# A sixth seven-product pair in five gate and up units, and where the unit before is turned back

## The chip, the cores and the metric

One core of a Trainium2 chip runs the whole program. TensorE (PE, with its weight loads PEld) multiplies, VectorE (DVE) and ScalarE (ACT) work on what it reads and leaves, GpSimd (POOL) and SyncE (SP) issue DMAs. The metric is the device time of one execution in microseconds (us). Lower is better.

## What is computed

The reference is a decoder layer on 16 + 256 tokens of width 2048: a gated feed-forward block (FFN1), attention beside a short convolution, a gated merge, a second feed-forward block (FFN2) and a norm. The change concerns FFN2, and a part of what it does is put into FFN1's time:

```python
D_MODEL = 2048
SEQ = 256
D_FF = ((8 * D_MODEL // 3 + 255) // 256) * 256
...
def swiglu_ffn(h, w_gu, w_down):
    gate, up = jnp.split(h @ w_gu, 2, axis=-1)
    return (jax.nn.silu(gate) * up) @ w_down
...
    h = rms_norm(s, norm_ffn2[layer])
    s = s + 0.5 * swiglu_ffn(h, ffn2_w_gu[layer], ffn2_w_down[layer])
```

D_FF is 5632. Inputs and outputs are float32.

## The kernel before

**Products.** Every float32 operand is kept as a high part and a rest, and a product is three matmuls: high by high, rest by high, high by rest (L593, L594, L595), each 128x128 by 128x512. The weights are split for that on the chip: ACT writes the high part `wh` (L498), DVE subtracts it and writes the rest `wl` (L499). `wh` and `wl` have four buffers each for tiles of 128x1024; tiles of 128x512 have buffers apart. PE's use of a tile is recorded three wide tiles behind its split (AHEAD).

**Units and pairs.** FFN2's gate and up projection works in 11 units of 512 gate and 512 up columns. The units stand in thirds (0 to 3, 4 to 7, 8 to 10), and behind each third come two down projections, one for each half of the output. In a unit the 16 chunks of the inner dimension are taken in 8 pairs. The two token halves by the pair's two chunks, times the two chunks by the two column groups (gate and up), is a product of 2x2 blocks. Its eight block products are made directly, or seven others from which the same result is put together:

- D, direct: 8 products, two weight tiles of 128x1024, from one load of 128x2048.
- S, seven products, with the sums of weights made on DVE out of the load (L632, L633, L634).
- P, seven products, with the sums of weights read from DRAM, where they were put earlier (`made`): a load of 128x1536 (L615) and two of 128x1024, `t24` and `t13` (L619, L620). Four tiles: 128x512, then three of 128x1024.

A seven-product pair also needs four sums of activations, with a high part and a rest (`Mixed.sum_of_parts` and `combine`, L546 to L566).

**The plan.** A plan names the kind of each pair, the pairs behind which one half of the unit before is turned back, and where an S pair's weight sums are made. Units 1 to 10 have `FFN2 = ("DDPPDSPP", (1,), {(4, 1): 5}, ())`, unit 0 has a plan of its own. Eight banks of PSUM hold the sums 1 to 7 and x of a unit. A direct pair adds to 2, 3, 4 and x, a seven-product pair to 1 to 7, and a sum is ready behind its last product. Then `done` (L679) takes it out: x by an ACT copy (L682), 3 and 1 are kept or copied, and DVE puts the others together (L692 to L703). This goes on in the next unit's first pairs, and ends with two scalar_tensor_tensor (L716), which write the activation `cup`.

**Turning back.** `cup` is turned by four transposes on PE for each half (L729, `mt_ps`), into a bank of its own, and split into the activation tile `m` on ACT and DVE (L733, L734).

**Making.** The sums of P pairs are made during FFN1, in pieces of half a pair: a fetch on POOL (L302), three adds on DVE (L306 to L308) and a store on POOL (L314). `tick` starts a step of this with every fifth call (TICKS), for a fetch and for the add and store of the piece three ahead of it. Before, MADE lists 44 pairs, which is 88 pieces.

**The order.** The program is a recording, and a scheduler sets each engine's order; a step that is written behind a pair may come later on its engine, where its bank or input is there. SP issues the loads of units in its own order, with three buffers for `st`, three for `t13` and two for `t24`.

Of the kernel before, what the change touches and what calls it, by code (L numbers as in the profile page):

```python
# [9 lines left out]
F32 = mybir.dt.float32  # L10
# [5 lines left out]
P = 128  # L16
# [4 lines left out]
F = 5632  # L21
DC = D // P
GC = 4
GW = GC * P
# [12 lines left out]
PIECE = 320  # L37
# [10 lines left out]
B_PLAN = ("DSDSDSDS", (2, 4), {(0, 1): 1, (2, 1): 3, (4, 1): 5, (6, 1): 7}, ())  # L48
FFN2_FIRST = ("DDDPDPPP", (1,), {}, ())
FFN2 = ("DDPPDSPP", (1,), {(4, 1): 5}, ())  # L50
OUT_FIRST = ("DDSDSDSD", (1,), {(1, 1): 2, (3, 1): 4, (5, 1): 6}, ())
OUT = ("DDDDSDSD", (), {(3, 1): 4, (5, 1): 6}, ())
DOWN_FIRST = ("DDDDSDSD", (1,), {(3, 1): 4, (5, 1): 6}, ())
# [4 lines left out]
TICKS = 5  # L58
MAKE_AHEAD = 3
MAKE_BUFS = N_AUX + 2  # L60
MADE = [(u, p) for u in range(F // GW) for p, kind in enumerate((FFN2 if u else FFN2_FIRST)[0]) if kind == "P"]


@with_exitstack
def decoder_layer(ctx: ExitStack, tc: tile.TileContext, t, out):
    nc = tc.nc
# [12 lines left out]
    def wide(shape, name):  # L79
        return tmp.tile(shape, F32, tag="wide", bufs=4, name=name)  # L80
# [38 lines left out]
    def load_vectors():  # L119
# [7 lines left out]
        out=mask[:, T - P :],  # L127
        in_=mask[:, T - P :],
# [25 lines left out]
    class Act:  # L154


        def __init__(self, name, chunks, width, wide_slots=(), piece=None):
            self.width, self.lead = width, 0 if piece is None else piece - width
            self.tiles = []
            for g in range(chunks // 2):  # L160
                if g in wide_slots:
                    w = piece or width
                    raw = apool.tile([P, 4 * PIECE], F32R, tag="big", bufs=N_BIG, name=f"{name}{g}")
                    self.tiles.append(raw[:, : 4 * w].rearrange("p (c l w) -> p c l w", c=2, l=2))
                else:
                    self.tiles.append(apool.tile([P, 2, 2, width], F32R, tag="act", name=f"{name}{g}"))

# [104 lines left out]
    side = []  # L272
# [42 lines left out]

    for n, (u, p) in enumerate(MADE):
        spare.extend(Making(n, u, p, k) for k in range(2))
# [212 lines left out]
    class Mixed:  # L530
# [22 lines left out]
        def combine(self, p, f, pool=None):  # L553
            a11, a12, a21, a22 = (f[:, c, i * P : (i + 1) * P] for i in range(2) for c in range(2))
            q = tmp.tile([P, 4, P], F32, tag="sc", name="sums")
            nc.vector.tensor_sub(q[:, 0, :], a21, a22)
            nc.vector.tensor_sub(q[:, 1, :], q[:, 0, :], a11)
            nc.vector.tensor_sub(q[:, 2, :], a11, a21)
            nc.vector.tensor_add(q[:, 3, :], a12, q[:, 1, :])
            if pool is None:  # L560
                sp = (aux if self.in_aux else apool).tile([P, 4, 2, P], F32R, tag="act", name=f"sp{p}")
            else:
                sp = pool.tile([P, 4, 2, P], F32R, tag="norm", bufs=1, name=f"sp{p}")
            nc.scalar.copy(out=sp[:, :, 0, :], in_=q)
            nc.vector.tensor_sub(sp[:, :, 1, :], q, sp[:, :, 0, :].bitcast(F32))
            self.sums[p] = [[sp[:, k, lo, :] for lo in range(2)] for k in range(4)]  # L566
# [142 lines left out]
    def gate_up_mix(plan, a, rtok, w_gu, g, m, gi):  # L709


        def end(gt, up):
            for i in range(2):
                r = rtok[:, i : i + 1]
                nc.scalar.activation(gt[:, i, :], gt[:, i, :], AF.Silu, scale=r)
                nc.vector.scalar_tensor_tensor(  # L716
                    out=up[:, i, :], in0=up[:, i, :], scalar=r, in1=gt[:, i, :], op0=ALU.mult, op1=ALU.mult
                )
            for k in range(2):
                later.append(lambda k=k: back(m, 2 * gi + k, up, k))  # L720

        mixed(plan, a, w_gu[g], "pg", end, made[g])

    def back(act, g, mt, k):

        pt = bank("mt_ps")
        for c in range(2):
            for i in range(2):
                nc.tensor.transpose(  # L729
                    pt[:, (2 * c + i) * P : (2 * c + i + 1) * P], mt[:, i, (2 * k + c) * P : (2 * k + c + 1) * P], ident  # L730
                )
        tl, f = act.tiles[g], pt.rearrange("p (c t) -> p c t", c=2)
        nc.scalar.copy(out=tl[:, :, 0, :], in_=f)  # L733
        nc.vector.tensor_sub(tl[:, :, 1, :], f, tl[:, :, 0, :].bitcast(F32))  # L734
# [43 lines left out]
    for half in halves:  # L778
        m = gate_up(h1, half, t["ffn1_w_gu"], norm1, 0, before1 if half is halves[0] else None)
# [201 lines left out]
    for g in range(2):  # L981
# [7 lines left out]
        if g == 0:  # L989
# [13 lines left out]
            half = len(units) // 2  # L1003
# [89 lines left out]
    h3 = Act("h3", DC, SEQ, range(4, NH))  # L1093
    hn = Mixed(h3, G_FFN2, False)
    rtok3 = const.tile([P, 2], F32, name="rtok3")
# [102 lines left out]
    side.append(lambda: mo.sum_of_parts(6))  # L1198
    add_mix(OUT_FIRST, mo, w_out, 0, 0, 1.0, "", out_done(0))
    add_mix(OUT, mo, w_out, 0, 1, 1.0, "", out_done(1))  # L1200
# [33 lines left out]
    w_gu, w_down, w_last = t["ffn2_w_gu"], t["ffn2_w_down"], t["ffn2_w_down_last"]  # L1234
    thirds = [list(range(0, 4)), list(range(4, 8)), list(range(8, ng))]
    for half in thirds:
        m = Act("m", len(half) * GC, SEQ, range(4))
        for gi, g in enumerate(half):
            gate_up_mix(FFN2 if g else FFN2_FIRST, hn, rtok3, w_gu, g, m, gi)
        final = half is thirds[-1]  # L1240
        if final:
            for q in range(2):
                nc.gpsimd.dma_start(
                    out=gfin[q],
                    in_=t["norm_final"][q * W2 : (q + 1) * W2].rearrange("(o d) -> o d", o=1).to_broadcast([P, W2]),
                )
        ma = Mixed(m, 0, True)
        for u in range(2):

            last_y = []  # L1250

            def score(i, q, u=u, f0=0, f1=GW, last_y=last_y):
                fs, k = slice(q * GW + f0, q * GW + f1), u * 2 + q
                end = k == 3 and i
                v, n = sT[i][u][:, fs], f1 - f0
                sq = wide([P, GW], "fsq")
                at = k + 1 if end and f0 else k
                nc.scalar.activation(sq[:, :n], v, AF.Square, accum_out=fss[:, i, at : at + 1])
                if end and not f0:
                    last_y.append(wide([P, GW], "fy"))  # L1260
                y = last_y[0][:, f0:f1] if end else v
                nc.vector.tensor_mul(y, v, gfin[u][:, fs])
                if k == 1 and i:

                    nc.scalar.activation(fr[:, i, 3:4], fss[:, i, 1:2], AF.Sqrt)
                if (end and not f0) or (k == 2 and not i):
                    finish_part(i)
                if k == 3 and f1 == GW:
                    finish(i, last_y[0] if i else y)

            def down(i, q, ps, f0=0, f1=GW, part=False, u=u, final=final, score=score):
                v = sT[i][u][:, q * GW + f0 : q * GW + f1]
                nc.vector.scalar_tensor_tensor(
                    out=v, in0=ps[:, : f1 - f0], scalar=0.5, in1=v, op0=ALU.mult, op1=ALU.add
                )
                if final and not part:
                    score(i, q, f0=f0, f1=f1)

            ops = [(m, 0)] * 2
            chunks = list(range(len(half) * GC))  # L1280
            if final and u == 0:
                side.append(lambda: None)
                side.extend(lambda p=p: ma.sum_of_parts(p) for p in (3, 5))
                add_mix(
                    DOWN_LAST, ma, w_down, half[0] * GC, u, 0.5, "side",
                    lambda score=score: side.extend(
                        lambda iq=iq: [score(*k) for k in iq] for iq in (((0, 0), (1, 0)), ((0, 1),), ((1, 1),))
                    ),
                )
            elif u == 0:  # L1290
                side.extend([lambda: None] * 2)
                side.extend(lambda p=p: ma.sum_of_parts(p) for p in (4, 6, 2))
                add_mix(DOWN_FIRST, ma, w_down, half[0] * GC, u, 0.5, "dma", lambda: None)
            elif not final:
                add_mix(DOWN, ma, w_down, half[0] * GC, u, 0.5, "dma", lambda: None)
            else:
                linear_tok(ops, w_last, chunks, 0, "pd", down, hold=HOLD, side_at=(1, 2, 3, 4, 5))
# [22 lines left out]
def _laid_out(np, inputs):  # L1320
# [8 lines left out]
    for name in ("ffn1_w_gu", "ffn1_w_down"):  # L1329
# [15 lines left out]
            np.stack([_quarter(w[2 * p * P : 2 * (p + 1) * P], u * GW + k * GW // 2, GW // 2) for k in range(2)])  # L1345
            for u, p in MADE
        ]
# [37 lines left out]
```

## Time and profile before

| what | before |
| --- | --- |
| median of 3 runs | 2138.32 us (2136.31 to 2138.91) |
| the profiled execution's own time | 2139.45 us |
| its span | 2137.2 us |
| granted clock, mean | 0.999 |
| HBM read | 478.45 MB |
| DMA, mean | 249 GB/s |

Times in rows of the profile count from the span's start. The rows of a timeline give the start, the duration of one record (of the group, where several stand in a row), the engine, the line, the operation and what is written from what. The records of one engine overlap a little: the next one starts before the record of the one ahead ends. FFN1 fills the first part of the span, FFN2 begins at about 1435 us. Units 5 and 6 are the stretches from 1733.02 to 1774.11 and from there to 1815.20, unit 8 that from 1941.29 to 1981.41.

### The profile page before, as it was taken

Reading aid. Unit: us, or ns where it says so; the run is one execution under the profiler, and the core shown is the slowest. Engines: PE = TensorE matmul, PEld = TensorE weight load, DVE = VectorE, ACT = ScalarE, POOL = GpSimd, SP = SyncE. Lnnn points to the kernel's source line nnn. Section 1 sums busy time; section 2 is a strip of 40 time slices with the busy share of each in tenths; the row PEclk is TensorE's granted clock in tenths of the full one; section 3 lists DMA queues with packets and bytes.
Section 4 is the critical chain, followed back from the end, with each engine's and each line's share of the span. In section 5 each row is a group of like instructions: output and inputs, shape, how many; then the busy total and the mean of one; then the engine's idle time right before and its main releaser. Section 6 shows DMA issues by size and latency. Waiting matters only on the chain.

```text
span 2137.2 us, 33274 instructions
## 1 busy us (share of the span) xinstructions
PE 2122.1 (99%) x13120; PEld 1916.5 (90%) x13120; DVE 1718.6 (80%) x2358; ACT 1123.4 (53%) x1420; POOL 126.7 (6%) x201
## 2 busy tenths in 40 slices
PE   8999999999999999999999999999999999999998
PEld 8999999999999998899998888887888888888887
DVE  7777776677776668967888888999999889998997
ACT  6444443344444445645545555557665567655665
POOL 0111111111111000000000000000000000000000
PEclk9999999999999999999999999999999999999999
DMA  7898888889888545544455555567875978668863
GB/s 279 315 321 322 322 324 317 317 317 328 315 313 323 188 166 192 181 172 150 147 182 193 201 201 189 206 217 244 284 272 198 291 270 295 243 223 302 293 226 138
DMA packets 98364, 533.04 MB, mean 249 GB/s; under 512 B 11680, under 2 KB 11936, under 8 KB 56224
## 3 DMA queue, kind: packets, MB, share of 16 engines
q1 hardware_dynamic: 69696, 432.72, 56.9%
q0 software_dynamic: 27936, 97.53, 13.7%
q8 instruction: 102, 1.67, 0.3%
q10 hardware_dynamic: 576, 0.67, 0.1%
q14 instruction: 54, 0.44, 0.1%
HBM read 478.45 MB, written 48.23 MB: 246 GB/s over the span
## 4 chain that ended last, share of the span: by engine, by line
PE 97%; DMA 1%; ACT 1%; DVE 1%; issue 0%; SPq 0%; ACTq 0%; DVEq 0%
PE pg L593 6%; PE pg L595 6%; PE pg L594 6%; PE pd L397 4%; PE pd L395 4%; PE pd L396 4%; PE pu L397 4%; PE pu L395 4%; PE pu L396 4%; PE pg L397 4%; PE pg L396 4%; PE pg L395 4%; PE pd L593 4%; PE pd L595 4%; PE pd L594 4%; PE g L595 2%
## 5 line engine op out<-in xcount | busy, mean ns | idle before, releaser
L384 DVE TENSOR_TENSOR wl<-st,wh 128x1024 fp32r<-128x1024 f32 (+1 forms) x329 | 400.5, 1221 | 256.6 <-ACT wh L379 256.4
L379 ACT CAST wh<-st 128x1024 fp32r<-128x1024 f32 (+1 forms) x328 | 343.3, 1048 | 485.4 <-PE pu L396 144.4
L499 DVE TENSOR_TENSOR wl<-st,wh 128x1024 fp32r<-128x1024 f32 (+1 forms) x424 | 462.3, 1104 | 55.1 <-ACT wh L498 50.8
L498 ACT CAST wh<-st 128x1024 fp32r<-128x1024 f32 (+1 forms) x424 | 394.1, 955 | 180.6 <-PE pdx L594 29.9
L498 ACT CAST wh<-t 128x1024 fp32r<-128x1024 f32 x188 | 193.9, 1052 | 233.2 <-DVE t L634 174.6
L499 DVE TENSOR_TENSOR wl<-t,wh 128x1024 fp32r<-128x1024 f32 x188 | 225.2, 1223 | 55.8 <-ACT wh L498 51.9
L395 PE MATMUL pg<-h,wh 128*128 128x272 f32 x704 | 201.1, 287 | 2.7 <-ACT h L211 1.5
L397 PE MATMUL pd<-mh,wl 128*128 128x272 f32 x704 | 203.1, 288 | 0.0
L397 PE MATMUL pu<-h,wl 128*128 128x272 f32 x704 | 201.8, 287 | 0.6 <-DVE wl L384 0.6
L395 PE MATMUL pd<-mh,wh 128*128 128x272 f32 x704 | 202.2, 287 | 0.0
L395 PE MATMUL pu<-h,wh 128*128 128x272 f32 x704 | 201.9, 287 | 0.0
L396 PE MATMUL pu<-h,wh 128*128 128x272 f32 x704 | 201.7, 287 | 0.0
L396 PE MATMUL pg<-h,wh 128*128 128x272 f32 x704 | 200.8, 287 | 0.0
L396 PE MATMUL pd<-ml,wh 128*128 128x272 f32 x704 | 200.8, 285 | 0.0
L397 PE MATMUL pg<-h,wl 128*128 128x272 f32 x704 | 199.9, 287 | 0.4 <-DVE wl L384 0.3
L593 PE MATMUL pg<-wh,h 128*128 128x512 f32 x366 | 142.9, 391 | 0.8 <-ACT wh L498 0.8
L595 PE MATMUL pg<-wl,h 128*128 128x512 f32 x366 | 143.3, 393 | 0.0
L594 PE MATMUL pg<-wh,h 128*128 128x512 f32 x366 | 142.6, 390 | 0.0
L395 PEld LDWEIGHTS pg<-h,wh 128*128 128x128 f32 x704 | 132.4, 188 | 3.4 <-ACT h L211 1.8
L396 PEld LDWEIGHTS pd<-ml,wh 128*128 128x128 f32 x704 | 133.5, 190 | 0.0
L397 PEld LDWEIGHTS pu<-h,wl 128*128 128x128 f32 x704 | 132.6, 188 | 0.8 <-DVE wl L384 0.8
L397 PEld LDWEIGHTS pg<-h,wl 128*128 128x128 f32 x704 | 131.6, 188 | 1.2 <-DVE wl L384 1.0
(383 smaller groups left out, 4985.8 us busy)
## 6 DMA issues: line engine op xcount, KB each, us to landing
st<-in_ffn_w_gu_dram SPq DMA_DIRECT2D x128, 1024.0 KB, 7.3
st<-in_ffn_w_down_dram SPq DMA_DIRECT2D x82, 1024.0 KB, 5.4
mk<-in_ffn_made_of_dram POOLq DMA_DIRECT2D x88, 512.0 KB, 8.6
made<-mk POOLq DMA_DIRECT2D x88, 512.0 KB, 6.1
t<-made SPq DMA_DIRECT2D x88, 512.0 KB, 5.7
st<-in_ffn_w_gu_dram SPq DMA_DIRECT2D x44, 768.0 KB, 5.3
st<-in_w_in_dram SPq DMA_DIRECT2D x32, 1024.0 KB, 4.8
st<-in_w_gate_dram SPq DMA_DIRECT2D x32, 1024.0 KB, 4.8
```

What stands on the lines that cost most here:

```text
L379: nc.scalar.copy(out=wh[:, :m, :], in_=sw)
L384: last_wl[:] = [nc.vector.tensor_sub(wl[:, :m, :], sw, wh[:, :m, :].bitcast(F32)).ins]
L395: nc.tensor.matmul(a, wh[:, i, f], act.part(c, 0, t0, t1), start=first, stop=False)
L396: nc.tensor.matmul(a, wh[:, i, f], act.part(c, 1, t0, t1), start=False, stop=False)
L397: nc.tensor.matmul(a, wl[:, i, f], act.part(c, 0, t0, t1), start=False, stop=last)
L498: part_last[:] = [nc.scalar.copy(out=wh, in_=src).ins]
L499: part_last.append(nc.vector.tensor_sub(wl, src, wh.bitcast(F32)).ins)
L593: nc.tensor.matmul(ps[k], hi, wh, start=first, stop=False)
L594: nc.tensor.matmul(ps[k], lo, wh, start=False, stop=False)
L595: nc.tensor.matmul(ps[k], hi, wl, start=False, stop=left[k] == 0)
```

## The change

Units 6 to 10 get a plan of their own, in which pair 1 is a P pair too, and in which the halves of the unit before are turned back behind pair 2 and not behind pair 1. The list of sums made ahead grows by the five pairs, from 88 pieces to 98. The activation sums of pair 1 are made in the first third's second down projection, and are kept in columns of four tiles of `h3` that are allocated and not used: a tile of 128x1280 holds 4 x 256 columns of activations.

```diff
+FFN2_MORE = ("DPPPDSPP", (2,), {(4, 1): 5}, ())
...
-MADE = [(u, p) for u in range(F // GW) for p, kind in enumerate((FFN2 if u else FFN2_FIRST)[0]) if kind == "P"]
+MORE_IN = (6, 7, 8, 9, 10)
+
+
+def _unit_plan(u):
+    return FFN2_MORE if u in MORE_IN else FFN2 if u else FFN2_FIRST
+
+
+MADE = [(u, p) for u in range(F // GW) for p, kind in enumerate(_unit_plan(u)[0]) if kind == "P"]
...
-            self.tiles = []
+            self.tiles, self.rest = [], []
...
                     self.tiles.append(raw[:, : 4 * w].rearrange("p (c l w) -> p c l w", c=2, l=2))
+                    self.rest.append(raw[:, 4 * w : 4 * PIECE])
...
+            if pool is self.act:
+                self.sums[p] = []
+                for k in range(4):
+                    sp = self.act.rest[k][:, : 2 * P].rearrange("p (l t) -> p l t", l=2)
+                    nc.scalar.copy(out=sp[:, 0, :], in_=q[:, k, :])
+                    nc.vector.tensor_sub(sp[:, 1, :], q[:, k, :], sp[:, 0, :].bitcast(F32))
+                    self.sums[p].append([sp[:, lo, :] for lo in range(2)])
+                return
...
-            gate_up_mix(FFN2 if g else FFN2_FIRST, hn, rtok3, w_gu, g, m, gi)
+            gate_up_mix(_unit_plan(g), hn, rtok3, w_gu, g, m, gi)
...
             elif not final:
+                if half is thirds[0]:
+                    side.extend((lambda: None, lambda: hn.sum_of_parts(1, h3)))
                 add_mix(DOWN, ma, w_down, half[0] * GC, u, 0.5, "dma", lambda: None)
```

Lines behind the new ones move: the split is L507 and L508 in the changed kernel, a product L610 to L612, the copy of x L699, the taking out L709 to L720, the scalar_tensor_tensor L733, a transpose L746, its split L750 and L751, the loads L632, L636 and L637, an S pair's sums L649 to L651. The orders that follow are those of the built programs.

DVE at the start of unit 7, from the split of its first tile (the first row) to the two scalar_tensor_tensor. In the kernel before:

```order
L499 TENSOR_TENSOR wl<-st,wh 128x1024
L692 TENSOR_TENSOR cgate<-pg_18038,cup 128x512
L694 TENSOR_TENSOR u2x<-pg_18152,cup 128x512
L499 TENSOR_TENSOR wl<-st,wh 128x1024
L696 TENSOR_TENSOR cgate<-pg_18046,u2x 128x512
L499 TENSOR_TENSOR wl<-st,wh 128x1024
L698 TENSOR_TENSOR cup<-pg_18163,u2x 128x512
L702 TENSOR_TENSOR cgate<-pg_18167,cgate 128x512
L699 TENSOR_TENSOR cup<-cup,u2x 128x512
L499 TENSOR_TENSOR wl<-st,wh 128x1024
L700 TENSOR_TENSOR cup<-pg_18042,cup 128x512
L703 TENSOR_TENSOR cup<-cup,pg_18167 128x512
```

In the changed kernel, from the second split of the unit on:

```order
L508 TENSOR_TENSOR wl<-st,wh 128x1024
L713 TENSOR_TENSOR cgate<-pg_18134,u2x 128x512
L508 TENSOR_TENSOR wl<-st,wh 128x512
L508 TENSOR_TENSOR wl<-st,wh 128x1024
L715 TENSOR_TENSOR cup<-pg_18197,u2x 128x512
L719 TENSOR_TENSOR cgate<-pg_18201,cgate 128x512
L716 TENSOR_TENSOR cup<-cup,u2x 128x512
L508 TENSOR_TENSOR wl<-t_18425,wh 128x1024
L717 TENSOR_TENSOR cup<-pg_18130,cup 128x512
L720 TENSOR_TENSOR cup<-cup,pg_18201 128x512
L508 TENSOR_TENSOR wl<-t_18424,wh 128x1024
L733 SCALAR_TENSOR_TENSOR cup<-cup,rtok_14394,cgate 128x512 x2
```

Pair 1's four tiles (128x512, then three of 128x1024, the last two from `t24` and `t13`) stand between the same operations where two of 128x1024 stood.

PE where unit 7 turns back the first half of unit 6 (`mt_ps`; `h` with a number is a tile of activations, `sp` their sums, `pg` with a number a bank). In the kernel before, in pair 1:

```order
L595 MATMUL pgx<-wl,h_14322 128x512
L593 MATMUL pg_18395<-wh,h_14322 128x512
L594 MATMUL pg_18395<-wh,h_14322 128x512
L729 MATMUL mt_ps<-ident,cup 128x128
L595 MATMUL pg_18395<-wl,h_14322 128x512
L593 MATMUL pg_18399<-wh,h_14322 128x512
L594 MATMUL pg_18399<-wh,h_14322 128x512
L729 MATMUL mt_ps<-ident,cup 128x128 x3
L595 MATMUL pg_18399<-wl,h_14322 128x512
```

In the changed kernel, in pair 5, behind the last product of x:

```order
L612 MATMUL pgx<-wl,h_14390 128x512
L610 MATMUL pg_18496<-wh,sp_15328 128x512
L611 MATMUL pg_18496<-wh,sp_15328 128x512
L612 MATMUL pg_18496<-wl,sp_15328 128x512
L610 MATMUL pg_18541<-wh,h_14391 128x512
L746 MATMUL mt_ps<-ident,cup 128x128 x4
L611 MATMUL pg_18541<-wh,h_14391 128x512
L612 MATMUL pg_18541<-wl,h_14391 128x512
```

The first four transposes moved from pair 1 to the fourth matmul behind x; the second four, which stood at the start of pair 2, stand 13 matmuls further on, in pair 5 too.

ACT at pair 5 of unit 7, with the copy that frees the bank of x. In the kernel before:

```order
L498 CAST wh<-t_18490 128x1024
L498 CAST wh<-t_18489 128x1024
L498 CAST wh<-st 128x1024
L682 COPY u2x<-pgx 128x512
L498 CAST wh<-st 128x512
```

In the changed kernel:

```order
L507 CAST wh<-t_18578 128x1024
L507 CAST wh<-t_18577 128x1024
L699 COPY u2x<-pgx 128x512
L507 CAST wh<-st 128x512
L507 CAST wh<-st 128x1024
L750 CAST m_17345<-mt_ps 128x2x256
L507 CAST wh<-t_18642 128x1024
```

The copy moved ahead of pair 6's first cast, and the split of the turned tile came to pair 6.

## Prediction

> **What bounds the kernel now.** I read the page first: the engines' busy time and the chain of work that ended last.
>
> ```profile
> span 2137.2 us, 33274 instructions
> PE 2122.1 (99%) x13120; PEld 1916.5 (90%) x13120; DVE 1718.6 (80%) x2358; ACT 1123.4 (53%) x1420; POOL 126.7 (6%) x201
> PE 97%; DMA 1%; ACT 1%; DVE 1%; issue 0%; SPq 0%; ACTq 0%; DVEq 0%
> ```
>
> TensorE is busy for 99% of the span and makes 97% of the chain. A matmul that goes is time that goes, as long as nothing else starts to hold PE up. Then the table by stretches: unit 6, unit 8, and two windows of FFN1's second down projection.
>
> ```profile
> core 0: us, PE busy (x) PEld busy (x) DVE busy (x) ACT busy (x) POOL busy (x), PEclk, DMA share, GB/s
> 1774.11:1815.20 41.09, 41.09 (x187) 33.98 (x185) 37.51 (x42) 27.52 (x32) 0.00 (x0) 1.00 0.81 283
> 1941.29:1981.41 40.12, 40.12 (x178) 33.23 (x177) 32.68 (x35) 25.86 (x29) 3.49 (x4) 1.00 0.91 292
> 700.00:750.00 50.00, 50.00 (x406) 50.00 (x405) 30.95 (x47) 23.60 (x35) 0.00 (x0) 1.00 0.50 179
> 750.00:800.00 50.00, 50.00 (x406) 50.00 (x405) 30.59 (x47) 24.31 (x34) 0.00 (x0) 1.00 0.50 170
> ```
>
> PE has no idle time in any of them, and its granted clock is 1.00. Unit 8 turns nothing back, so it is 177 matmuls in 40.12 us: 0.2267 us each. Unit 6 has the same 177 and eight transposes: (41.09 - 40.12) / 8 = 0.12 us each. What is near the limit beside PE is VectorE: 37.51 of 41.09 us.
>
> **The matmuls that go.** A direct pair is 8 products, a seven-product pair 7, and a product is 3 matmuls. Five units lose 3 each: 15 x 0.2267 = **3.40 us**, 0.16% of the run. That is all the change can win: the other instructions of PE stay, the eight transposes of a unit too. The Trainium skill's page "TensorE: Matmul & The Clock Gate" (section "Back-to-back issue gap") gives a stream of weight loads and 512-wide matmuls about 131 ns each, and 216 ns for the bare gap; by these the gain would be 2.0 or 3.2 us, but the row of unit 8 has 0.2267, between records that lie next to each other too, and the row decides.
>
> **DVE in the five units.** Pair 1 had two splits of 128x1024 and has three and one of 128x512 now. A record is longer than the pitch, so I take starts of neighbours:
>
> ```profile
> start us, us, engine line op out<-in xcount [idle before <-releaser]
> 1770.41 1.23 DVE L499 TENSOR_TENSOR wl<-st,wh 128x1024 fp32r<-128x1024 f32 x1
> 1771.66 0.69 DVE L692 TENSOR_TENSOR cgate<-pg,cup 128x512 f32<-128x512 f32 x1
> 1772.27 0.69 DVE L694 TENSOR_TENSOR u2x<-pg,cup 128x512 f32<-128x512 f32 x1
> 1772.87 1.22 DVE L499 TENSOR_TENSOR wl<-st,wh 128x1024 fp32r<-128x1024 f32 x1
> 1774.01 0.69 DVE L696 TENSOR_TENSOR cgate<-pg,u2x 128x512 f32<-128x512 f32 x1
> 1774.61 1.22 DVE L499 TENSOR_TENSOR wl<-st,wh 128x1024 fp32r<-128x1024 f32 x1
> ...
> 1781.60 1.42 DVE L716 SCALAR_TENSOR_TENSOR cup<-cup,rtok,cgate 128x512 f32<-128x512 f32 x2
> 1782.92 2.36 DVE L499 TENSOR_TENSOR wl<-t,wh 128x1024 fp32r<-128x1024 f32 x2
> ```
>
> So 1.14 us for 1024 wide, 0.60 for 512, 0.66 for one of the two L716. The change adds 1.14 + 0.60 = 1.74 us: 37.51 becomes 39.25, of 41.09 - 0.68 = 40.41 us, or 97%. A mean says little; what counts is the tightest place. It is the start of a unit, where DVE also puts the unit before together. With t = 0 at PE's first matmul of the unit (1774.11), the first split ends at 1771.64, t = -2.47. From there to the split of pair 2's second tile the order of the changed kernel has ten 512-wide operations (8 of L709 to L720, and 2 splits), five splits 1024 wide and the two L733: 10 x 0.60 + 5 x 1.14 + 1.32 = 13.0, so that split ends at t = 10.5. PE first wants it with its third matmul: behind 24 + 21 + 3 + 2 = 50 matmuls, t = 11.3. Spare: **0.8 us**, the smallest in the unit. The tiles ahead have more, and behind it a seven-product pair costs DVE 3 x 1.14 + 0.60 = 4.0 us against 21 x 0.2267 = 4.76 of PE, so the lead grows again. Cost 0. Bounds: 0, and, if each of the five splits took its full record of 1.23, 0.45 more, which still fits.
>
> **Turning back.** Behind a seven-product pair 1 all eight PSUM banks hold sums, so the transposes get a bank only when x is ready, at the end of pair 4, and ACT has copied it out. The order shows them there, in pair 5, and the copy (L682, now L699) directly behind the cast of pair 5's last tile. Here is that place in unit 5, ACT, PE and DVE:
>
> ```profile
> 1758.14 2.00 ACT L498 CAST wh<-t 128x1024 fp32r<-128x1024 f32 x2 [3.98 <-DVE t L634]
> 1760.05 1.05 ACT L498 CAST wh<-st 128x1024 fp32r<-128x1024 f32 x1
> 1761.00 0.57 ACT L682 COPY u2x<-pgx 128x512 f32<-128x512 f32 x1
> ```
>
> ```profile
> 1759.60 0.39 PE L595 MATMUL pgx<-wl,h 128*128 128x512 f32 x1
> 1759.83 0.39 PE L593 MATMUL pg<-wh,sp 128*128 128x512 f32 x1
> ```
>
> ```profile
> 1753.87 1.22 DVE L632 TENSOR_TENSOR t<-st 128x1024 f32<-128x1024 f32 x1
> ...
> 1757.34 0.69 DVE L634 TENSOR_TENSOR t<-t,st 128x512 f32<-128x512 f32 x1
> ...
> 1761.50 1.83 DVE L499 TENSOR_TENSOR wl<-st,wh 128x1024 fp32r<-128x1024 f32 x2
> ```
>
> The copy may now start at 1760.05 and ends 0.57 later, 1760.62. PE comes to the first transposes 4 matmuls behind 1759.83, at 1760.74. A handover costs about 0.11 (L634 ends at 1758.03, ACT starts at 1758.14), so PE waits 0 to 0.1. If the copy stood behind the next cast as before, it would end at 1761.57 and PE would wait 0.83 or more. The second four need the first four's subtraction, which stands behind the two splits of 1761.50: about 1763.24 + 0.69 = 1763.9, against PE at 1759.83 + 17 x 0.2267 + 4 x 0.12 = 1764.2. So 0 to 0.1 there too. Units 6, 7, 9 and 10 turn back: 4 x 0.1 = **+0.4** (bounds 0 and 3.3).
>
> **Loads.** Pair 1 gets 0.79 MB more in each unit, 1.05 becoming 1.83. The one that could be late is pair 5's raw weights: they take the buffer that pair 2's leave (three of them), so they are issued when pair 2's second split ends, t = 10.5. L649 (L632 before) wants them where it stood, 1759.83 - 1753.87 = 5.96 ahead of PE's pair 5: 111 x 0.2267 - 5.96 = 19.2. That gives the load 8.7 us. The first row is from issue to landing in units 5 to 7 and the projections behind, the second at the start of unit 8, where the POOL queue still adds the down projection:
>
> ```profile
> DMA to landing us min/median/max: 4.0/5.0/8.5
> ...
> DMA to landing us min/median/max: 8.0/9.0/10.0
> ```
>
> At 5.0 there are 3.7 us to spare, at 10.0 it is 1.3 late. Only unit 8 can see that, and it has no transposes behind it. I take **+0.2**, bounds 0 and 1.3. The Trainium skill ("DMA: Bandwidth & Descriptors", section "Anatomy of one DMA — SWDGE (gpsimd) path") fits a DMA as 2.0 us and bytes / 436e3; its 1 MB would land in an estimated 4.4 us whatever else runs, and no load would be late. The rows of unit 8 have twice that, so the rule is no bound here.
>
> **The extra sum and the ten extra pieces.** The sum for pair 1 is one 512-wide add and eight 128-wide operations on DVE:
>
> ```profile
> 1619.29 0.28 DVE L556 TENSOR_TENSOR sums<-mf 128x128 f32<-128x128 f32 x1
> 1619.49 0.29 DVE L558 TENSOR_TENSOR sums<-mf 128x128 f32<-128x128 f32 x1
> ```
>
> 0.60 + 8 x 0.20 = 2.2 us, in a down projection of which DVE used this much:
>
> ```profile
> 1648.30:1688.00 39.70, 39.70 (x177) 32.88 (x176) 35.16 (x39) 20.84 (x23) 3.56 (x4) 1.00 0.88 280
> ```
>
> 4.5 us are free there and PE never waits; cost 0, and 2.2 if none of it is hidden. The making of the sums grows by ten pieces, each a fetch on POOL, three adds on DVE and a store:
>
> ```profile
> 695.59 0.69 DVE L306 TENSOR_TENSOR mk<-mk 128x512 f32<-128x512 f32 x1
> 696.31 0.42 DVE L307 TENSOR_TENSOR mk<-mk 128x256 f32<-128x256 f32 x1
> 696.77 0.43 DVE L308 TENSOR_TENSOR mk<-mk 128x256 f32<-128x256 f32 x1
> ...
> 650.00:700.00 50.00, 50.00 (x407) 50.00 (x406) 35.97 (x52) 19.97 (x23) 7.19 (x11) 1.00 0.83 299
> ```
>
> From 695.59 to the end of L308 at 697.20 it is 1.6 us each and 16 in all, in FFN1's second down projection from about 700 on, where DVE uses 31 of 50 us and the DMA engines half. In the 50 us ahead of that, the last row, the pieces of before ran beside the same matmuls, and PE had no idle time. I take +0.1, bounds 0 and 2.
>
> **Sum.** -3.40 + 0.4 + 0.2 + 0.1 = -2.7 us. The profiled execution took 2139.45 (2137.2 and 2.2 around it): 2136.75. It lies 1.1 above the median of the runs, 2138.32; from that I predict **2135.6**. A measurement of this kernel can tell about 0.2% (4.3 us) from no change, and the whole gain is less than that.
>
> **Rivals.** (1) *Half the gain is eaten* (0.22): the copy of x comes late by half the 0.83 above, or unit 8's load and the made pieces cost their upper bounds. 4 x 0.4 + 1.3 + 0.5 = 3.4: between -1.5 and +0.5, about 2138. Against it: every chain above fits, if by 0.1 to 0.8 us. (2) *Slower: pair 5's load comes late in each unit* (0.10). Its window shrank since its buffer now comes free behind a third split tile, and it competes with the added 0.79 MB. Lateness goes straight through L649 to L651, the casts of pair 5 and the copy of x to the transposes, so PE waits for all of it in the four units that turn back. At 10.0 us from issue to landing it is 1.3 x 4 + 0.7 - 3.4 = +2.5, at 10.5 us +4.5; from 9.4 us on the change loses (0.7 x 4 + 0.7 is 3.5). For it: the rows of unit 8, and a DMA share of 0.81 that grows. Against: the median of 5.0. (3) *DVE becomes the bound* (0.05): if 0.8 us of spare at pair 2 isn't there because a load of pair 1 or the first split comes a microsecond later, PE waits what is missing, some 0.5 in each of five units: -0.2, 2138. (4) *It does more than it says* (0.03): nothing in the trace could give more than 3.40, since PE has no idle time in these stages to win.
>
> **How the numbers follow.** Forecast, -3.4 to -1.5 and the scatter of the runs (2136.3 to 2138.9 before): 0.60, with the range 2134 to 2137. With the rivals I go from 2133.8 to 2141, which leaves out the far end of rival 2 and of the scatter. Faster by over 0.2% needs 4.3 us, more than is removed, so only scatter gives it: 0.08. Slower by over 0.2% is rival 2 beyond 10.4 us and what I haven't seen: 0.09. Within 0.2%: 0.83.
>
> **What would show it.** Units 7 and 10 should take 40.4 to 40.6 us with PE busy throughout and DVE at 39 us. Unit 8's 40.12 should become 39.4. A gap on PE ahead of the first transposes, in pair 5, ended by ACT's copy of x, is rival 1; if L649 waits there for its load, rival 2. A gap at pair 1 or 2 ended by a split is rival 3. PE gaps between 700 and 790 us would be the made pieces. What would make all of it wrong is an order on the chip other than the built one, or splits that slow down when DVE has no pauses.

## The result and the profile after

| what | before | after |
| --- | --- | --- |
| median of 20 runs each | 2137.97 us | 2134.33 us |
| ratio | | 0.9985, 95% interval 0.9978 to 0.9991 |
| the profiled execution's own time | 2139.45 us | 2134.09 us |
| its span | 2137.2 us | 2132.3 us |

The ratio stands for 3.2 us less, between 1.9 and 4.7. The interval leaves out "no change", and the gain is smaller than 0.2% (4.3 us). One of the 20 runs of before took 3546.05 us, the others 2136.10 to 2140.54; it counts in the median and not in the ratio. 2135.6 was forecast.

The page of the changed kernel, with the lines that answer to those of before:

```profile
span 2132.3 us, 33396 instructions
PE 2119.2 (99%) x13105; PEld 1914.7 (90%) x13105; DVE 1741.4 (82%) x2407; ACT 1131.8 (53%) x1434; POOL 139.3 (7%) x221
PE 97%; DMA 1%; DVE 1%; ACT 1%; issue 0%; SPq 0%; ACTq 0%; DVEq 0%
```

PE has 15 matmuls less and is the bound as before. DVE has 49 operations more (2407 against 2358), POOL 20 DMAs. Units 6 to 10 and two windows of FFN1's second down projection, in the table by stretches (the columns as in the prediction):

```profile
1772.40:1812.84 40.44, 40.44 (x183) 33.37 (x182) 38.81 (x44) 28.96 (x35) 0.00 (x0) 1.00 0.89 316
1812.84:1853.28 40.44, 40.44 (x183) 33.37 (x182) 38.97 (x44) 28.75 (x34) 0.00 (x0) 1.00 0.75 264
1938.29:1977.73 39.44, 39.44 (x175) 32.67 (x174) 34.51 (x37) 27.05 (x31) 3.52 (x4) 1.00 0.95 317
1977.73:2018.20 40.47, 40.47 (x184) 33.37 (x182) 38.82 (x44) 28.97 (x35) 0.00 (x0) 1.00 0.90 325
2018.20:2058.64 40.44, 40.44 (x183) 33.37 (x182) 38.97 (x44) 28.76 (x34) 0.00 (x0) 1.00 0.75 260
695.00:745.00 50.00, 50.00 (x405) 50.00 (x404) 39.91 (x67) 24.24 (x34) 7.52 (x12) 1.00 0.88 304
745.00:795.00 50.00, 50.00 (x406) 50.00 (x405) 33.97 (x55) 22.42 (x31) 4.70 (x7) 1.00 0.74 259
```

The table covers five units without a pause on PE, each 0.62 to 0.68 us shorter than before, and two windows in which DVE and the DMA engines do a good deal more than the 31 of 50 us and 0.50 of before, with PE busy throughout.

The spans differ by 4.9 us, which is more than 15 matmuls can be. So the first question is where the time went. For every trace I took PE's first matmul of each unit; a unit lasts from its own to the next one's, and the first column is the time at which the query projection behind FFN1 begins:

| trace | begin | units 0+1 | 4 | 5 | 6 | 7 | 8 | 9 | 10 |
| --- | --- | --- | --- | --- | --- | --- | --- | --- | --- |
| before | 819.10 | 85.91 | 40.12 | 41.09 | 41.09 | 41.10 | 40.12 | 41.09 | 41.09 |
| changed | 817.75 | 85.55 | 40.12 | 41.09 | 40.44 | 40.45 | 39.44 | 40.47 | 40.44 |
| before, again | 816.94 | 88.59 | 40.12 | 41.09 | 41.09 | 41.10 | 40.12 | 41.09 | 41.09 |
| changed, again | 817.13 | 85.19 | 40.12 | 41.09 | 40.43 | 40.47 | 39.44 | 40.48 | 40.43 |
| made only | 817.19 | 88.61 | 40.12 | 41.09 | 41.09 | 41.10 | 40.12 | 41.09 | 41.09 |
| turn behind pair 1 | 816.48 | 88.58 | 40.12 | 41.08 | 40.48 | 40.45 | 39.44 | 40.48 | 40.45 |
| later turn alone | 816.87 | 85.56 | 40.12 | 41.08 | 41.16 | 41.16 | 40.12 | 41.17 | 41.19 |
| one addition more | 816.26 | 86.89 | 40.12 | 41.09 | 40.40 | 40.42 | 39.44 | 40.43 | 40.44 |
| two more | 817.16 | 85.33 | 40.12 | 41.09 | 40.40 | 40.59 | 39.44 | 40.44 | 40.61 |
| four more | 816.98 | 86.73 | 40.12 | 41.09 | 40.44 | 41.84 | 39.44 | 40.44 | 41.85 |
| units 4 to 10 | 816.33 | 87.33 | 39.44 | 40.73 | 40.45 | 40.42 | 39.44 | 40.44 | 40.44 |
| units 2 to 10 | 816.01 | 86.92 | 39.44 | 40.47 | 40.46 | 40.47 | 39.44 | 40.47 | 40.47 |
| D in unit 0 | 817.45 | 89.34 | 40.12 | 41.08 | 40.47 | 40.47 | 39.44 | 40.44 | 40.44 |
| both | 817.36 | 88.47 | 39.44 | 40.45 | 40.46 | 40.41 | 39.44 | 40.44 | 40.48 |

Units 6 to 10 give 0.65 + 0.65 + 0.68 + 0.62 + 0.65 = 3.25 us. The other 1.7 us of the two traces lie in the first column (1.35) and in units 0 and 1 (0.36). The experiments ask whose they are.

### The profile page after: what moved, and what is told of

It reads as the page before. It is cut to its first block, busy times and chain, and to the rows that moved or that the text cites. A ratio compares the mean times of both kernels' runs of the same rounds, so it can differ in the third digit from the quotient of the medians.

```text
span 2132.3 us, 33396 instructions
## 1 busy us (share of the span) xinstructions
PE 2119.2 (99%) x13105; PEld 1914.7 (90%) x13105; DVE 1741.4 (82%) x2407; ACT 1131.8 (53%) x1434; POOL 139.3 (7%) x221
## 4 chain that ended last, share of the span: by engine, by line
PE 97%; DMA 1%; DVE 1%; ACT 1%; issue 0%; SPq 0%; ACTq 0%; DVEq 0%
PE pg L610 6%; PE pg L612 6%; PE pg L611 6%; PE pd L406 4%; PE pd L404 4%; PE pu L406 4%; PE pu L404 4%; PE pu L405 4%; PE pd L405 4%; PE pg L406 4%; PE pg L404 4%; PE pg L405 4%; PE pd L610 4%; PE pd L612 4%; PE pd L611 4%; PE g L611 2%
## 5 line engine op out<-in xcount | busy, mean ns | idle before, releaser
L508 DVE TENSOR_TENSOR wl<-st,wh 128x1024 fp32r<-128x1024 f32 (+1 forms) x424 | 458.1, 1095 | 46.9 <-ACT wh L507 42.9
L507 ACT CAST wh<-st 128x1024 fp32r<-128x1024 f32 (+1 forms) x424 | 390.4, 950 | 173.7 <-PE z L439 27.3
L507 ACT CAST wh<-t 128x1024 fp32r<-128x1024 f32 x198 | 204.5, 1052 | 228.7 <-DVE t L651 171.6
L508 DVE TENSOR_TENSOR wl<-t,wh 128x1024 fp32r<-128x1024 f32 x198 | 236.7, 1221 | 50.4 <-ACT wh L507 46.8
L611 PE MATMUL pg<-wh,h 128*128 128x512 f32 x371 | 144.9, 391 | 0.0
L610 PE MATMUL pg<-wh,h 128*128 128x512 f32 x371 | 144.9, 391 | 0.0
L612 PE MATMUL pg<-wl,h 128*128 128x512 f32 x371 | 144.5, 391 | 0.0
L404 PEld LDWEIGHTS pg<-h,wh 128*128 128x128 f32 x704 | 133.1, 190 | 2.2 <-ACT h L220 2.2
L405 PEld LDWEIGHTS pg<-h,wh 128*128 128x128 f32 x704 | 133.1, 190 | 0.0
```

Source lines behind the costliest of these rows:

```text
L404: nc.tensor.matmul(a, wh[:, i, f], act.part(c, 0, t0, t1), start=first, stop=False)
L405: nc.tensor.matmul(a, wh[:, i, f], act.part(c, 1, t0, t1), start=False, stop=False)
L507: part_last[:] = [nc.scalar.copy(out=wh, in_=src).ins]
L508: part_last.append(nc.vector.tensor_sub(wl, src, wh.bitcast(F32)).ins)
L610: nc.tensor.matmul(ps[k], hi, wh, start=first, stop=False)
L611: nc.tensor.matmul(ps[k], lo, wh, start=False, stop=False)
```

## The experiments

**1. The kernel before, once more.** No edit.

> The kernel before, unchanged, for a second trace. The changed kernel's trace was 4.95 us ahead at the end of unit 10, of which 1.35 were there before the query projection (819.10 against 817.75) and 0.36 more came in units 0 and 1 (85.91 against 85.55 us together). Theory A: these 1.71 us are the scatter of two places that wait for loads, and belong to no part of the change; then the second trace of before differs from the first by 0.3 us or more at one of them, while units 5 to 10 come out at 41.09, 41.09, 41.09, 40.12, 41.09, 41.09 within 0.03. Theory B: the change wins them; then the second trace repeats 819.1 and 85.9 within 0.2.

2140.07 us, one run. Theory A holds, and more strongly than I had put it: the first column moved by 2.2 us without any edit, and units 0 and 1 by 2.7 us the other way. Over all traces the first column runs from 816.0 to 819.1. The unit times repeat to 0.01 us. So a difference of two single traces at such a place says nothing here below 3 us; the unit times and the medians of many runs do.

**2. The hidden parts alone.** The ten more pieces are made, and the sum of pair 1, but all units keep the old plan, so neither is used.

```diff
-            gate_up_mix(_unit_plan(g), hn, rtok3, w_gu, g, m, gi)
+            gate_up_mix(FFN2 if g else FFN2_FIRST, hn, rtok3, w_gu, g, m, gi)
```

> The changed kernel with the old plan in all units: the ten more pieces are made and the sum of pair 1 is made, and neither is used. Theory: both are hidden. FFN1's second down projection has no wait of PE beyond 0.5 us, the first third's second down projection stays at 41.48, units 6 to 10 at 41.09 and 40.12; against before 0.0 +- 0.1%. Rival (the pieces are not free, bounds of the prediction 0 to 2 us; the sum 0 to 2.2 us): one of these stretches is longer by over 0.2 us.

2137.68 us, ratio to before 0.9996 (0.9986 to 1.0005): no difference. Where the pieces now run:

```profile
700.00:750.00 50.00, 50.00 (x405) 50.00 (x405) 40.12 (x68) 24.25 (x34) 8.25 (x13) 1.00 0.88 303
750.00:800.00 50.00, 50.00 (x406) 50.00 (x405) 35.77 (x62) 24.70 (x35) 2.71 (x4) 1.00 0.68 237
```

DVE went from 31 to 40 and 36 of 50 us, PE kept 50.00. The projection with the extra sum takes 41.48 us in this trace and in the trace of before. Both parts are hidden.

**3. The pair without the later turn.**

```diff
-FFN2_MORE = ("DPPPDSPP", (2,), {(4, 1): 5}, ())
+FFN2_MORE = ("DPPPDSPP", (1,), {(4, 1): 5}, ())
```

> The sixth pair without the later turn: plan DPPPDSPP with the turn written behind pair 1, as before. The built order then puts the eight transposes into pairs 1 and 2, where they take the last two banks, and both splits of the turned tile on DVE behind pair 2's second split. Theory (banks and DVE): the banks come back about 1.2 us behind t = 10.5, and the splits of pair 2 come 1.2 us later than in the changed kernel, where there were 0.7 to spare; PE waits 0.5 to 1.5 us in units 6, 7, 9 and 10, which take 41.0 to 42.0 instead of 40.45; unit 8 stays at 39.44. Rival (the place of the turn costs nothing): 40.45 within 0.1.

2134.35 us, ratio to before 0.9981 (0.9970 to 0.9991). My theory fell: the units take 40.45 to 40.48, and the later turn is worth nothing that these runs can tell. PE in unit 6 of this kernel, where the transposes stand among the products of pairs 1 and 2:

```profile
1781.91 0.39 PE L611 MATMUL pg<-wh,sp 128*128 128x512 f32 x1
1782.14 0.39 PE L610 MATMUL pg<-wh,h 128*128 128x512 f32 x1
...
1782.59 0.27 PE L746 MATMUL mt_ps<-ident,cup 128*128 128x128 f32 x1
...
1783.40 0.93 PE L746 MATMUL mt_ps<-ident,cup 128*128 128x128 f32 x7
...
1784.86 0.39 PE L612 MATMUL pg<-wl,sp 128*128 128x512 f32 x1
...
1787.92 0.40 PE L612 MATMUL pg<-wl,sp 128*128 128x512 f32 x1
```

```profile
1786.19 2.35 DVE L508 TENSOR_TENSOR wl<-t,wh 128x1024 fp32r<-128x1024 f32 x2
```

The product at 1781.91, pair 2's first, lacks its third matmul, the one with `wl`. It comes at 1784.86, behind matmuls that were ready. The scheduler had put the waiting matmuls back and others ahead of them. And the eight transposes, 0.97 us of PE, now stand ahead of pair 2's later tiles, so PE comes to these later too. The rest of pair 2's third tile, the second row, is split 1.4 us later in the unit than in the changed kernel, and ends at 1787.41; PE wants it at 1787.92. Late splits met late matmuls, and nothing stood still.

**4. The later turn without the pair.**

```diff
-FFN2_MORE = ("DPPPDSPP", (2,), {(4, 1): 5}, ())
+FFN2_MORE = ("DDPPDSPP", (2,), {(4, 1): 5}, ())
...
-                if half is thirds[0]:
+                if False:
```

> The later turn alone: the old plan DDPPDSPP with the turn behind pair 2 in units 6 to 10, no pair more, no sum of pair 1. The built order puts the transposes into pair 2. Theory: the gain is matmuls alone, so units 6, 7, 9 and 10 stay at 41.09 within 0.1, unit 8 at 40.12. Rival (part of the 0.65 us of a unit comes from turning back at a calmer place): they come out shorter than 41.0.

One run, 2137.14 us. The units that turn back take 41.16 to 41.19, 0.06 to 0.10 more than before. Turning back later gains nothing in itself. With experiment 2, only the matmuls are left as the source of the gain.

**5. The changed kernel, once more.** No edit.

> The changed kernel, unchanged, for a second trace and more times. Theory: the gain is 3.24 us, five times 0.65 in units 6 to 10, and what the two traces differ by beside that is the wait for loads in units 0 and 1 (85.55 to 88.61 us together in five traces so far) and the first 40 us. Then units 6 to 10 repeat 40.44, 40.45, 39.44, 40.47, 40.44 within 0.03, whatever units 0 and 1 take, and the ratio is 0.9985 +- 0.0007. Rival (the change also wins in units 0 and 1): they take 85.6 again and the ratio is 0.998 or less.

2133.65 us, ratio 0.9982 (0.9973 to 0.9991). The units repeat within 0.02. Units 0 and 1 took 85.19, the least of all traces, so by this run alone theory and rival cannot be told apart; but the kernel of experiment 3 has all of the pair's work too and took 88.58 there. That place varies with the execution.

**6 to 8. How much more can DVE take?** The sum 2 of the unit before is written two, three or five times, with the same values, at the start of units 6, 7, 9 and 10:

```diff
-                nc.vector.tensor_add(gt[:, 0, :], ps, up[:, 0, :])
+                for _ in range(1 + more_dve):
+                    nc.vector.tensor_add(gt[:, 0, :], ps, up[:, 0, :])
...
-        mixed(plan, a, w_gu[g], "pg", end, made[g])
+        mixed(plan, a, w_gu[g], "pg", end, made[g], 1 if g in (5, 6, 8, 9) else 0)
```

with 2 and 4 in place of the 1 for the other two.

> The changed kernel with one more 512-wide addition on DVE (the sum 2 is written twice, with the same values) at the start of units 6, 7, 9 and 10. Theory (DVE has 0.69 us to spare at pair 2's second split, measured as the time from its end to PE's first use): 0.60 fits, the units stay at 40.45 within 0.05. Rival (DVE is the bound already): 0.6 longer, 41.05.

> The same with two more additions, 1.20 us: theory 1.20 - 0.69 = 0.5 us of waiting in each of units 6, 7, 9 and 10, so 40.95; rival (DVE is the bound already) 41.65; rival (the order hides it) 40.45.

> The same with four more additions, 2.40 us: theory 2.40 - 0.69 = 1.7 us of waiting in each of units 6, 7, 9 and 10, so 42.15 (the gain of 0.65 of a unit is lost from about 1.3 us, two additions, on); rival (DVE is the bound already) 42.85; rival (the order hides it) below 41.0.

2133.88, 2135.21 and 2138.64 us, one run each. 0.60 us fits, as the theory had it. 1.20 us costs nothing in units 6 and 9 and 0.14 to 0.17 in units 7 and 10, not 0.5. 2.40 us costs nothing in 6 and 9 and 1.4 in 7 and 10, together 2.8 and not 6.8 us. So the 0.69 us at pair 2 is no fixed limit: as in experiment 3 the built order moves PE's third matmuls back. What decides is the lead that DVE brings in from the unit before. Units 6 and 7 with four more additions:

```profile
1772.80:1813.24 40.44, 40.44 (x183) 33.38 (x182) 39.10 (x46) 28.57 (x35) 0.00 (x0) 1.00 0.82 286
1813.24:1855.08 41.84, 41.28 (x183) 33.12 (x182) 40.72 (x48) 27.78 (x34) 0.00 (x0) 1.00 0.83 286
```

In unit 6 DVE does 39.10 us of work in 40.44 and leaves the rest to unit 7. This is the first split of unit 7, in the changed kernel and with four more additions:

```profile
1809.14 1.22 DVE L508 TENSOR_TENSOR wl<-st,wh 128x1024 fp32r<-128x1024 f32 x1
```

```profile
1811.38 1.22 DVE L508 TENSOR_TENSOR wl<-st,wh 128x1024 fp32r<-128x1024 f32 x1
```

It ends 2.93 us ahead of PE's use in the one and 1.10 ahead in the other. Unit 6 with four more additions still has 2.93. Units 9 and 10 repeat 6 and 7: 2.93 and no loss, 1.11 and 1.4 us lost. With two more additions units 7 and 10 have 2.46 and 2.50, and lose 0.14 and 0.17. Where the lead is short, the wait does come at pair 2, when that pair's first split (it ended at about 1826.84) is late:

```profile
1826.39 0.39 PE L611 MATMUL pg<-wh,sp 128*128 128x512 f32 x1
1826.89 0.50 PE L612 MATMUL pg<-wl,sp 128*128 128x512 f32 x1
1827.60 0.50 PE L610 MATMUL pg<-wh,sp 128*128 128x512 f32 x1 [0.20 <-ACT wh L507]
```

From start to start that is 0.50 and 0.71 where 0.23 is usual. With the next start it is 0.9 us of waiting, and 0.4 more stand ahead of the second four transposes. The table counts only 0.56 of it as idle, since a record of 0.39 us covers a wait of up to 0.16. The change itself leaves 40.44 - 38.97 = 1.47 us of a unit free.

**9. The pair in units 4 to 10.**

```diff
-MORE_IN = (6, 7, 8, 9, 10)
+MORE_IN = (4, 5, 6, 7, 8, 9, 10)
```

> The sixth pair in units 4 to 10, 102 pieces. The sum of pair 1 is made in the projection just ahead of unit 4. Theory: units 4 and 5 gain like units 8 and 7, 0.68 and 0.65, to 39.44 and 40.44; 4.57 us in all against before, ratio 0.9979; the four more pieces of the making end about 37 us later and stay hidden. Rival (unit 4's start is too tight, since its loads compete with the additions of the projection, or the sum comes late): unit 4 at 40.0 or more.

2132.63 us, ratio to before 0.9978 (0.9969 to 0.9987). Unit 4 gains 0.68 as expected, unit 5 only 0.36. PE and ACT in pair 5 of unit 5:

```profile
1756.87 0.39 PE L610 MATMUL pg<-wh,h 128*128 128x512 f32 x1
1757.36 0.66 PE L746 MATMUL mt_ps<-ident,cup 128*128 128x128 f32 x4
```

```profile
1756.74 0.57 ACT L699 COPY u2x<-pgx 128x512 f32<-128x512 f32 x1
```

The copy of x ends at 1757.31 and the transposes, which could have begun 0.23 behind 1756.87, begin at 1757.36: 0.26 us of waiting for the bank. It is the mechanism of the prediction's first rival, at a third of the 0.83 that a copy behind the next cast would have cost, in one unit. The chain ahead of the copy is 0.28 us later in the unit than in unit 7 of the changed kernel, from pair 4's second cast on: by the profile it waits for PE's L612 here and for L611, one matmul earlier, there.

**10. The pair in units 2 to 10.** It needs the sum earlier and more pieces, so these are made at every fourth call:

```diff
-TICKS = 5
+TICKS = 4
...
-MORE_IN = (6, 7, 8, 9, 10)
+MORE_IN = (2, 3, 4, 5, 6, 7, 8, 9, 10)
...
+                        lambda: hn.sum_of_parts(1, h3),
...
-                if half is thirds[0]:
-                    side.extend((lambda: None, lambda: hn.sum_of_parts(1, h3)))
```

> The sixth pair in units 2 to 10, 106 pieces made at every fourth call and not every fifth, the sum of pair 1 made in the output projection ahead of unit 0. Theory: nine units gain 0.65, 5.9 us, ratio 0.9972, if the denser making stays hidden in FFN1 (every piece costs DVE 1.6 us, and the DMA engines were busy for 0.81 there). Rival (the denser making and the sum are not hidden): FFN1 up to the query projection grows by 2 us or more, or the output projection's second half is longer than 44.45, and the ratio is 0.998 or more.

2132.38 us, ratio 0.9978 (0.9969 to 0.9987). In units 2 and 3 it is 40.43 each (41.10 and 41.11 before), and units 2 to 10 gain 5.8 us; the making stays hidden (the query projection begins at 816.01), and so does the sum: from there to unit 0 it takes 620.72 us, against 620.63 in the trace of before. The median is 4.96 us below before's, where the changed kernel's were 3.64 and 3.63. By units this version is 2.6 us ahead of the change; the intervals of the runs overlap, so by runs that isn't shown.

**11 and 12. A direct pair in unit 0.** In most traces PE waits at the start of unit 1 for a load, and units 0 and 1 vary by 3 us. So I took one seven-product pair out of unit 0, in the changed kernel and in that of experiment 10:

```diff
-FFN2_FIRST = ("DDDPDPPP", (1,), {}, ())
+FFN2_FIRST = ("DDDPDPDP", (1,), {}, ())
```

> The changed kernel with one seven-product pair less in unit 0: DDDPDPDP and not DDDPDPPP. In ten traces units 0 and 1 took 85.2 to 88.6 us together; where unit 1's load of pair 1, issued at about 1480, landed in 5.1 us, PE waited 0.3 there, where it took 7.0 to 7.2, 2.3 to 2.4. At the end of unit 0 the splits' lead on PE falls from 4.6 to 0.8 us over three seven-product pairs. Theory: DVE's lag there makes these loads late, three at once; with a direct pair, 1.74 us less for DVE and 0.79 MB less to load, the lead stays above 1.5, PE does not wait in unit 1, and units 0 and 1 take 83.5 to 84.5 us although unit 0 has 3 matmuls more; units 6 to 10 unchanged; 1 to 4 us less than the changed kernel. Rival (loads land late there whatever DVE does): 86 to 89 us, and 0.7 us more than the changed kernel.

> Both: the sixth pair in units 2 to 10 with the denser making, and DDDPDPDP in unit 0. Theory: the two gains add, 5.83 us of units 2 to 10 and 1 to 4 of units 0 and 1, ratio against before 0.9955 to 0.9975. Rival (loads of unit 1 late as in the kernel before): 0.9978 or more.

2136.77 us, ratio 0.9992 (0.9983 to 1.0001), and 2135.05 us, ratio 0.9984 (0.9975 to 0.9992). The further gain isn't there: the medians are 1.59 and 3.31 us below before's, where those without the edit are 3.6 and 4.96, though the intervals overlap. In unit 1 PE doesn't wait for the load, as the theory said; but it also comes there some 4 us later. Units 0 and 1 took 89.34 and 88.47 us together, against 85.55 and 85.19 in the changed kernel's traces and 86.92 in that of experiment 10. The loss is in unit 0. There, in the first of the two, PE and ACT at the end of pair 6:

```profile
1476.54 0.39 PE L612 MATMUL pgx<-wl,h 128*128 128x512 f32 x1
1478.32 0.66 PE L1133 MATMUL h_ps<-ident,sT 128*128 128x128 f32 x4 [1.40 <-ACT u2x L699]
1479.54 0.51 PE L610 MATMUL pg<-wh,h 128*128 128x512 f32 x1 [0.56 <-ACT h L1137]
```

```profile
1476.74 1.04 ACT L507 CAST wh<-st 128x1024 fp32r<-128x1024 f32 x1 [1.67 <-PE pgx L611]
1477.69 0.58 ACT L699 COPY u2x<-pgx 128x512 f32<-128x512 f32 x1
```

With the last direct pair at 6, x keeps its bank until there. The last transposes of the activations (L1133) wait for that bank, and here the copy of x stands behind a cast. This is the first rival's mechanism in full: PE waits 1.40 us, of which the copy itself is 0.58 and its delay behind the cast 0.76 (1477.69 against the end of x's last product, 1476.93), and 0.56 more for the next input. The other trace has the same two waits. Three more matmuls add 0.7, and in the first trace the clock fell too (below). I had overlooked that moving the last D moves the bank.

## Why the prediction was right

- **The gain is 15 matmuls of 0.2267 us: right.** 3.40 was the term, and unit 8 shows it bare, 40.12 - 39.44 = 0.68. Experiments 2 and 4 leave the matmuls as the only source that was found.
- **The costs: mechanisms right, sizes too large.** I charged 0.7 us and the runs show 0.15 (3.40 - 3.25). The term that was mis-sized is the turning back, +0.4. This is the place in unit 7 of the changed kernel:

```profile
1838.00 0.39 PE L610 MATMUL pg<-wh,sp 128*128 128x512 f32 x1
...
1838.91 0.64 PE L746 MATMUL mt_ps<-ident,cup 128*128 128x128 f32 x4
```

```profile
1836.36 2.00 ACT L507 CAST wh<-t 128x1024 fp32r<-128x1024 f32 x2 [3.97 <-DVE t L651]
1838.26 0.58 ACT L699 COPY u2x<-pgx 128x512 f32<-128x512 f32 x1
```

  The copy ends 0.84 us behind pair 5's first matmul, 0.79 was worked out; PE comes at 0.91, as worked out. It is in time by 0.07, and a unit pays 0.03 to 0.06 us (against 39.44 + 0.97 for the transposes = 40.41), not 0.1. The +0.2 for unit 8's load and the +0.1 for the pieces are 0: unit 8 has no pause, and experiment 2 shows the pieces free. For unit 8 it was the issue that the working had wrong, and not the landing. Its load of pair 5 took 10.0 us, the bound with 1.3 us of lateness; the first row is that load, the second the L649 that reads it:

```profile
DMA to landing us min/median/max: 10.0/10.0/10.0
...
1957.49 1.22 DVE L649 TENSOR_TENSOR t<-st 128x1024 f32<-128x1024 f32 x1
```

  It was issued at 1946.65, 8.4 us into the unit and not 10.5, and landed at 1956.69, 0.8 ahead of L649. The 10.5 holds for a unit at whose start DVE puts another one together, and no gate and up unit stands right before unit 8.
- **DVE's tightest place: right in size, wrong as a limit.** 0.8 us to spare at pair 2's second split were forecast:

```profile
1821.67 1.82 DVE L508 TENSOR_TENSOR wl<-st,wh 128x512 fp32r<-128x512 f32 x2
```

```profile
1824.18 0.39 PE L612 MATMUL pg<-wl,h 128*128 128x512 f32 x1
```

  The split ends at 1823.49 and is used at 1824.18: 0.69. DVE has 38.97 us of work in the unit, 39.25 were forecast. But experiments 6 to 8 show that it is no fixed limit: the order gives way, and 1.20 us more cost no more than 0.17 in a unit. Only at 2.40, and only where DVE's lead into the unit had fallen to 1.10 us, did PE wait there for 0.9.
- **Pair 5's load: right.** It was to have 8.7 us. In units 6, 7, 9 and 10 it took 7.0, 4.8, 7.0 and 6.2. All raw loads of units 4 to 7 and the projections behind landed in

```profile
DMA to landing us min/median/max: 4.1/5.3/10.4
```

  and no L649 of these units waits. The slower rival didn't occur.
- **The turn behind pair 2.** The prediction didn't claim a gain from it, only that the banks force the transposes into pair 5. Behind pair 1 it goes as well (experiment 3), so they don't force it: 0.04 us in a unit at most.
- **The number.** 2135.6 was 2138.32 - 2.7. The base had the median of three runs; of twenty it is 2137.97 (0.35 less), and the costs were 0.55 too high. Of the 1.3 us between forecast and measurement that is 0.9; the other 0.4 is within the interval and may be units 0 and 1. That 2134.33 came to lie inside 2134 to 2137, by 0.3 us, is luck in part: the same kernel's second series, in experiment 5, has 2133.65, beside a median of before that is 0.7 lower too.

## What to carry to other kernels

Where PE is never idle, count the matmuls that go, find the one or two places where a new wait could start, and work those out from neighbouring starts; the sum was good to 0.6 us in 2138. When a split would be late by less than a tile, look at the order before pricing it: a scheduler that can put other matmuls first can make the price vanish, until the lead that the engine brings into the unit is used up. When a product is moved to another pair, ask which bank it then holds for longer. And before reading a difference of two single traces, take the same kernel twice: here single places moved by 2 to 3 us without any edit.

## What the runs showed of the hardware

A short pause can cost more than itself. In unit 1 PE waits for one load, which landed 7.2 us behind its issue in the second trace of before and 5.1 us in the second trace of the changed kernel, with the same three loads issued one behind the other. The first line is from the one, the second from the other:

```profile
DMA to landing us min/median/max: 7.2/7.2/7.2
```

```profile
DMA to landing us min/median/max: 5.1/5.1/5.1
```

With 5.1 us PE waited 0.1. With 7.2 it had no matmul for 2.0 us, and then, in the second trace of before:

```profile
1488.92 0.71 PE L593 MATMUL pg<-wh,h 128*128 128x512 f32 x1 [2.00 <-ACT wh L498]
```

```profile
1486.00:1488.00 2.00, 0.92 (x5) 0.42 (x3) 0.81 (x2) 0.17 (x1) 0.00 (x0) 1.00 0.98 390
1488.00:1490.00 2.00, 1.08 (x3) 0.89 (x4) 1.10 (x1) 2.00 (x3) 0.00 (x0) 0.76 0.58 240
1490.00:1492.00 2.00, 2.00 (x7) 1.52 (x6) 2.00 (x4) 2.00 (x3) 0.00 (x0) 0.50 0.04 18
1492.00:1494.00 2.00, 2.00 (x9) 1.66 (x8) 2.00 (x3) 0.90 (x2) 0.00 (x0) 0.89 0.84 246
```

The granted clock fell to 0.50 for 3.4 us (by the shares of the table 0.96 + 2.00 + 0.44), in which a matmul took 0.43 us. Units 0 and 1 came to 88.59 us. Three traces with such a pause (2.2 to 2.4 us from start to start) have the lower clock and take 88.6; four others with 2.1 to 2.4 keep 1.00 and take 86.7 to 87.3, like this one, that of the pair in units 4 to 10:

```profile
1486.00:1488.00 2.00, 0.53 (x3) 0.10 (x1) 0.42 (x1) 0.51 (x1) 0.00 (x0) 1.00 1.01 409
1488.00:1490.00 2.00, 1.42 (x6) 1.20 (x7) 1.44 (x2) 2.00 (x4) 0.00 (x0) 1.00 0.47 194
```

The two waits of experiments 11 and 12, 1.40 and 0.56 us, were followed by a clock of 0.50 in the first trace and of 1.00 throughout in the second. So whether a pause of 2 us halves the clock differs from one execution to the next. It costs 1.3 to 1.9 us more; 3.4 us at half the clock are 1.7 us of matmuls. The Trainium skill ("TensorE: Matmul & The Clock Gate", section "What's actually happening") has the clock fall behind at least one idle window of about 3.4 us; here 1.8 to 2.0 us of idle time were enough in three of seven traces. What makes that load land in 5 us in one execution and in 7 in the next stays open.
